# A masked softmax with lengths: masking 32 columns from the length on, with the tail filled by GpSimd

## The chip, the core and the metric

The kernel runs on one core of one Trainium2 chip. The metric is the device time of that core in microseconds (us): the median of several executions. The core has five engines that matter here: TensorE (PE), VectorE (DVE), ScalarE (ACT), GpSimd (POOL) and SyncE (SP), and 16 DMA engines that move data between the chip's main memory (HBM) and the on-chip memory (SBUF, 128 partitions). Engines run their own instruction streams and wait for one another through semaphores.

## What is computed

The input x is 16 x 8 x 256 x 256 in float32, with one length for each of the 16 batches. Each row of 256 columns gets a softmax over its first `length` columns; the columns behind are zero in the output.

```python
def reference(x, lengths):
    result = np.zeros_like(x)
    for b in range(batch):
        length = lengths[b]
        masked = x[b, :, :, :length].copy()
        masked = masked - np.max(masked, axis=-1, keepdims=True)
        exp_masked = np.exp(masked)
        result[b, :, :, :length] = exp_masked / np.sum(exp_masked, axis=-1, keepdims=True)
    return result
```

The lengths lie between 128 and 255. The draw that is timed has 188, 233, 229, 243, 195, 252, 165, 210, 222, 180, 209, 157, 159, 199, 214 and 248.

## The kernel before

A batch is 8 x 256 = 2048 rows, 16 on each of the 128 partitions: 16 x 256 float32, 16 KB on a partition and 2 MB in all. SBUF has `slots = 8` places for a batch (tile `xt`), and position b of the order uses slot b % 8. The order is batches 1, 2, 3, 15, then 4 to 14, and batch 0 last; `batch_of` maps positions to batches. `half`, `quarter` and `lump` are 8, 4 and 4 of a partition's 16 rows. Everything is written by hand with semaphores; no scheduler moves an instruction.

**Loads.** Position 0 is loaded by SP in two halves (L145). GpSimd loads positions 1 to 3 whole (L196), and then, in a loop over two parities, positions 4 to 15 (L205 to L211). For these it reads the length into a register (L210, by the helper at L135) and picks one of twelve loads by a tree of branches: `pick` has the widths 160, 168, ... 240 and 256, and its leaf loads only the first w columns of each row (L168). Before such a load GpSimd waits for the store that empties the slot (`s_st`, L209; the first four find it counted already by a seed) and for the landing of the load of the same parity before it (`s_sw`, L167). So two loads are under way at a time.

The columns w to 255 of the slot are not written by a narrow load. In slots 4 to 7 they are zeroed once at the start (L191, columns 160 to 255, four memsets); later they hold what the batch eight positions earlier left there, which are finite numbers.

**Mask.** For each position VectorE replaces t in columns 128 to 255 (`mid` to 255) by the smaller of t and `down + len_s` (L248, the function `clip`). `down` is -1e30 x (column + 0.5), `len_s` is 1e30 x length, so the sum is hugely negative from the column `length` on and hugely positive ahead of it. The function `mask` waits for the load and runs the clip over all 16 rows of a partition, 2048 elements (position 0 in two parts of 1024).

**Exponentials and sums.** ScalarE takes the exponential of the first 4 rows at once (L374), and of the other 12 one by one with their sums (L377). VectorE sums the first 4 rows (L269, `total`). No maximum is subtracted; at the end the sums are looked at, and if one lies outside a range (or a length is under 128) a slow path works all batches again. With this input it isn't taken.

**Division and stores.** VectorE multiplies each half of a batch by the reciprocal of its sums (L279 and L282, `divide`). Its order for position b is: divide the first half of b, mask b + 1, divide the second half of b, sum the lump of b + 1 (position 1 divides first what it can). SP stores the finished parts (L154): it waits for the part (`s_out`, L149) and, for positions 2 to 12, also for the complete store of position b - 2 (L153), so that two batches are in store at most; positions 13 to 15 wait for nothing else than their parts. At the end SP waits for all stores (L157 to L159, L407).

The helper `step` counts instructions of VectorE in the semaphore `s_v`; GpSimd waits for it at L188, ahead of its first memset of `xt` and of the loads of positions 1 to 3.

Of the kernel before, what the change touches and what calls it, by code (L numbers as in the profile page):

```python
# [9 lines left out]
F32 = mybir.dt.float32  # L10
BF16 = mybir.dt.bfloat16
I32 = mybir.dt.int32
ALU = mybir.AluOpType
AX = mybir.AxisListType.X
EXP = mybir.ActivationFunctionType.Exp
DVE = mybir.EngineType.DVE
# [5 lines left out]
def kernel(  # L22
# [6 lines left out]
    nc = tc.nc  # L29
    P = nc.NUM_PARTITIONS  # L30

    batch, heads, seq_q, seq_k = x.shape
    rows = heads * seq_q
    assert rows % P == 0
    nt = rows // P
# [10 lines left out]
    slots = 8  # L46
    ahead = 4
    assert ahead == 4 and slots == 8 and batch == 16

    def batch_of(pos):  # L50
        return pos + 1 if pos < ahead - 1 else {ahead - 1: 15, 15: 0}.get(pos, pos)
# [3 lines left out]
    low = widths[0]  # L55
    mid = seq_k // 2
    big = 1.0e30

    def parts(b):


        if b == 0:
            cuts = [0, 2, quarter, half, nt]
        elif b < 8:
            cuts = [0, half, half + quarter, nt]
        elif b < 13 or b == batch - 1:
            cuts = [0, half, nt]
        else:
            cuts = [0, nt]
        return [slice(i, j) for i, j in zip(cuts, cuts[1:])]  # L70

    pool = ctx.enter_context(tc.tile_pool(name="all", bufs=1))
    psum = ctx.enter_context(tc.tile_pool(name="psum", bufs=1, space=bass.MemoryType.PSUM))
    xt = pool.tile([P, slots, nt, seq_k], F32, name="xt")
    word64 = pool.tile([1, batch], mybir.dt.int64, name="word64")
    word = word64.bitcast(I32)
# [3 lines left out]
    len_s = pool.tile([P, batch], F32, name="len_s")  # L80
    iota_i = pool.tile([P, seq_k], I32, name="iota_i")
    down = pool.tile([P, seq_k], F32, name="down")
    row_sum = pool.tile([P, slots, nt], F32, name="row_sum")
    inv_sum = pool.tile([P, batch, nt], F32, name="inv_sum")
    warm = pool.tile([P, 1], F32, name="warm")
# [20 lines left out]
    with tc.tile_critical(no_gpsimd_drain=True):  # L106
# [9 lines left out]
        s_fill = sem("s_fill")  # L116
        s_v = sem("s_v")
        s_min = sem("s_min")
# [14 lines left out]
        def length(engine, at):  # L133

            return nc.values_load(  # L135
                at,
                engines=[engine],
                skip_runtime_bounds_check_because="compared with constants, never an address",
            )
# [3 lines left out]
        for h in range(2):  # L143
            s = slice(h * half, (h + 1) * half)
            nc.sync.dma_start(out=xt[:, 0, s], in_=x_f[batch_of(0), :, s]).then_inc(s_ld[h], 16)  # L145
        for b in range(batch):
            s_b = s_st[b % 2] if b < late else s_late if b < batch - 1 else s_last
            for s in parts(b):
# [3 lines left out]
                if 2 <= b < late and s.start == 0:  # L152
                    nc.sync.wait_ge(s_b, 64 * (b // 2 + 2))  # L153
                nc.sync.dma_start(  # L154
                    out=out_f[batch_of(b), :, s, :], in_=xt[:, b % slots, s, :]
# [7 lines left out]
        def pick(v, b, slot, par, ws, landed):  # L163

            if len(ws) == 1:
                w = ws[0]
                nc.gpsimd.wait_ge(s_sw[par], landed)  # L167
                nc.gpsimd.dma_start(  # L168
                    out=xt[:, slot, :, :w], in_=x_n[:, b, :, :w]
                ).then_inc(s_sw[par], 16)  # L170
                return
            m = (len(ws) - 1) // 2
            with nc.gpsimd.If(v <= ws[m]):
                pick(v, b, slot, par, ws[: m + 1], landed)
            with nc.gpsimd.Else():
                pick(v, b, slot, par, ws[m + 1 :], landed)
# [8 lines left out]
        nc.gpsimd.memset(ones_c, 1.0).then_inc(s_ones, 1)  # L185
        for par in range(2):
            nc.gpsimd.memset(seed[:, par : par + 1], 0.0).then_inc(s_st[par], 128)  # L187
        nc.gpsimd.wait_ge(s_v, 2)  # L188

        def fill(b):  # L190
            nc.gpsimd.memset(xt[:, b, :, low:], 0.0).then_inc(s_fill, 1)  # L191


        fill(ahead)
        for b in range(1, ahead):
            nc.gpsimd.dma_start(out=xt[:, b], in_=x_f[batch_of(b)]).then_inc(  # L196
                s_sw[b - 1] if b < 3 else s_ld[2], 16
            )
        nc.gpsimd.wait_ge(s_word, 16)
        for b in range(ahead + 1, slots):  # L200
            fill(b)
        nc.gpsimd.wait_ge(s_fill, slots - ahead)


        with nc.Fori(16, 16 * (batch // 2 - 1), 16, engines=[POOL]) as landed:  # L205
            for par in range(2):
                n = landed // 8 + (ahead - 2 + par)
                b = n % 15 if par == 1 else n
                nc.gpsimd.wait_ge(s_st[par], 4 * landed)  # L209
                v_len = length(POOL, word[0:1, bass.ds(2 * b, 1)])  # L210
                pick(v_len, bass.ds(b, 1), bass.ds(n % slots, 1), par, widths + [seq_k], landed)  # L211
# [11 lines left out]
        def step(ins):  # L223
            nonlocal v
            v += 1
            ins.then_inc(s_v, 1)
# [5 lines left out]
                out=down, in0=iota_i, scalar1=0.5, scalar2=-big, op0=ALU.add, op1=ALU.mult  # L232
            )
        )
        nc.vector.wait_ge(s_word, 16)
        nc.vector.tensor_copy(out=len_b, in_=word[:, ::2]).then_inc(s_lenb, 1)  # L236
        nc.vector.wait_ge(s_lenf, 1)
        step(
            nc.vector.tensor_scalar(  # L239
                out=len_s, in0=len_f, scalar1=big, scalar2=None, op0=ALU.mult  # L240
# [1 line left out]
        )  # L242
        nc.vector.wait_ge(s_v, v)

        def clip(b, s, lo, hi):

            t = xt[:, b % slots, s, lo:hi]
            return nc.vector.scalar_tensor_tensor(  # L248
                out=t,
                in0=down[:, None, lo:hi].to_broadcast([P, s.stop - s.start, hi - lo]),  # L250
                scalar=len_s[:, batch_of(b) : batch_of(b) + 1],
                in1=t,
                op0=ALU.add,
                op1=ALU.min,
            )

        def mask(b, s):
            if b == 0:
                nc.vector.wait_ge(s_ld[s.start // half], 16)
            elif b == ahead - 1:  # L260
                nc.vector.wait_ge(s_ld[2], 16)
            else:
                par = (b - 1 if b < ahead else b) % 2
                nc.vector.wait_ge(s_sw[par], 16 * max(b // 2, 1))
            clip(b, s, mid, seq_k).then_inc(s_min, 1)

        def total(b):
            nc.vector.wait_ge(s_lump, b + 1)
# [7 lines left out]
        def divide(b, h):  # L276
# [10 lines left out]
            ).then_inc(s_out, 1)  # L287

        mask(0, slice(0, half))
        mask(0, slice(half, nt))  # L290
        total(0)
        for b in range(batch):


            first = b != 1
            if first:
                divide(b, 0)
            if b + 1 < batch:
                mask(b + 1, slice(0, nt))
            if not first:  # L300
                divide(b, 0)
            divide(b, 1)
            if b + 1 < batch:
                total(b + 1)
# [14 lines left out]
        for k, (_, _, edge, op) in enumerate(checks):  # L319
            nc.vector.tensor_scalar(  # L320
                out=bad[:, k : k + 1],
                in0=ends[:, k : k + 1],
                scalar1=edge,
                scalar2=None,
                op0=op,
# [9 lines left out]
        with nc.vector.Else():  # L335
            with nc.Fori(0, batch, 1, engines=[DVE]) as i:
                nc.vector.wait_ge(g_ld, 16 * i + 16)
                nc.vector.scalar_tensor_tensor(
                    out=g_t,
                    in0=down[:, None, :].to_broadcast([P, nt, seq_k]),  # L340
                    scalar=len_s[:, bass.ds(i, 1)],
                    in1=g_t,
                    op0=ALU.add,
                    op1=ALU.min,
# [3 lines left out]
                    out=neg_max, in_=g_t, op=ALU.max, axis=AX, negate=True  # L348
# [5 lines left out]
                    out=g_t,  # L354
                    in0=g_t,
# [9 lines left out]
        with nc.Fori(0, batch // slots, 1, engines=[ACT]) as turn:  # L365
            for slot in range(slots):
                for h in range(2):
# [7 lines left out]
                    for j in range(h * half + lump * (1 - h), (h + 1) * half):  # L375
                        e = xt[:, slot, j, :]
                        ins = nc.scalar.activation(  # L377
                            out=e, in_=e, func=EXP, accum_out=row_sum[:, slot, j : j + 1]
# [5 lines left out]
        with nc.scalar.If(a_redo >= 1):  # L384
# [4 lines left out]
            with nc.Fori(0, batch, 1, engines=[ACT]) as i:  # L389
                nc.scalar.dma_start(out=g_t, in_=x_g[:, bass.ds(i, 1)]).then_inc(g_ld, 16)  # L390
                nc.scalar.wait_ge(g_v, 3 * i + 2)
                with nc.Fori(0, nt, 1, engines=[ACT]) as t:
                    e = g_t[:, bass.ds(t, 1), :]
                    nc.scalar.activation(
                        out=e,
                        in_=e,
# [41 lines left out]
```

## Time and profile before

| what | value |
|---|---|
| median of 3 runs | 154.53 us (154.44 to 154.55) |
| the profiled execution: from its first to its last instruction (span) | 152.8 us |
| between the span and the median of the runs | 1.7 us |
| VectorE busy | 134.6 us, 88% of the span |
| ScalarE busy | 95.1 us, 62% |
| GpSimd busy | 21.3 us, 14% |
| bytes moved by DMA | 61.57 MB, mean 403 GB/s |

The profiled execution is one run of its own and has no time beside its span; the time of the runs also has what lies ahead of the first and behind the last instruction. In rows of the profile, L282 is line 282 of the kernel; a row of instructions gives the line, the engine, the operation, output <- inputs with their shapes, then the busy time in us and the mean in ns of one, and the idle time before it with what ended it. "SPq" and "DVEq" are the sequencers of those engines, where waits, register instructions and DMA issues run, which are not counted as busy. A row of waits gives the waiter, what it waited for, us in total, times, and the longest. A row of stretches gives the window, its length, the busy time of PE, PEld, DVE, ACT and POOL with the number of instructions that began in it, the granted TensorE clock, the mean busy share of the 16 DMA engines (over 1 where packets overlap), and GB/s. q0 is the queue of GpSimd's loads, q1 that of SP's loads and stores.

### The profile page before, as it was taken

The numbers are of one execution on the slowest core, as the hardware profiler recorded it, in microseconds if no ns is written. First come the engines' busy times: TensorE is split into PE (matmuls) and PEld (weight loads), VectorE is DVE, ScalarE is ACT, GpSimd is POOL, SyncE is SP. The second block draws the span as 40 slices with busy tenths as digits, with TensorE's granted clock in tenths as the row PEclk, the third lists the DMA queues.
The fourth block names the chain that finished last, engine by engine and source line by source line (L and its number), as shares of the span: only waits on it lengthen the run. The fifth ranks groups of instructions, "written<-read, shape, count | busy, mean of one in ns | idle before, by whom it ended". The sixth has DMA issues, their size and how long they took to land.

```text
span 152.8 us, 818 instructions
## 1 busy us (share of the span) xinstructions
PE 0.3 (0%) x2; PEld 0.2 (0%) x2; DVE 134.6 (88%) x107; ACT 95.1 (62%) x402; POOL 21.3 (14%) x29
## 2 busy tenths in 40 slices
PE   0000000000000000000000000000000000000000
PEld 0000000000000000000000000000000000000000
DVE  1369999999999999999999999999999999999500
ACT  3096699339394967859393939577593939395000
POOL 4962110030303020030300220302000000000000
DMA  4999999999999999999999999999999999999994
GB/s 107 420 446 433 401 435 347 421 445 420 394 397 422 405 421 411 411 409 405 419 411 418 408 399 419 408 410 423 417 421 419 413 420 422 435 435 442 429 410 187
DMA packets 10646, 61.57 MB, mean 403 GB/s; under 512 B 898, under 2 KB 1010, under 8 KB 7058
## 3 DMA queue, kind: packets, MB, share of 16 engines
q1 hardware_dynamic: 5904, 35.65, 56.7%
q0 software_dynamic: 4736, 25.89, 41.9%
q14 instruction: 4, 0.03, 0.1%
q10 hardware_dynamic: 2, 0.00, 0.0%
HBM read 27.98 MB, written 33.55 MB: 403 GB/s over the span
## 4 chain that ended last, share of the span: by engine, by line
DVE 87%; DMA 5%; issue 1%; SPq 0%; PE 0%
DVE xt L282 48%; DVE xt L248 23%; DVE row_sum L269 12%; DMA xt<-in_x_dram 5%; DVE inv_sum L279 3%; DVE ends L317 0%; SPq L145 0%; DVE bad L320 0%; PE count L218 0%; DVE redo L328 0%; SPq L433 0%; SPq L106 0%
## 5 line engine op out<-in xcount | busy, mean ns | idle before, releaser
L377 ACT ACTIVATE xt<-xt 128x256 f32<-128x256 f32 x192 | 76.6, 400 | 0.2 <-DVE xt L248 0.2
L282 DVE TENSOR_TENSOR xt<-xt,inv_sum 128x2048 f32<-128x2048 f32 x32 | 73.3, 2292 | 1.1
L374 ACT ACTIVATE xt<-xt 128x1024 f32<-128x1024 f32 x16 | 16.9, 1056 | 42.8 <-DVE xt L248 42.8
L248 DVE SCALAR_TENSOR_TENSOR xt<-down,len_s,xt 128x2048 f32<-128x2048 f32 (+1 forms) x17 | 37.7, 2219 | 5.0 <-DMA xt<-in_x_dram 5.0
L377 ACT ACTIVATION_READ_ACCUMULATOR xt<-xt 128x1 f32 x192 | 35.9, 187 | 0.0
L168 POOL DMA_DIRECT2D xt<-in_x_dram x12 | 13.2, 1104 | 84.0 <-DMA xt<-in_x_dram 62.3
L269 DVE TENSOR_REDUCE row_sum<-xt 128x4 f32<-128x1024 f32 x16 | 19.4, 1210 | 0.0
L279 DVE RECIPROCAL inv_sum<-row_sum 128x8 f32<-128x8 f32 x32 | 6.3, 198 | 0.5
L191 POOL MEMSET xt<- 128x1536 f32 x4 | 5.4, 1398 | 1.1 <-DVE len_s L239 1.1
L361 ACT ACT_TABLE_LOAD x1 | 1.3, 1283 | 1.6 <-SPq L106 1.6
L196 POOL DMA_DIRECT2D xt<-in_x_dram x3 | 1.8, 590 | 0.0
L231 DVE TENSOR_SCALAR down<-iota_i 128x256 f32<-128x256 int32 x1 | 0.3, 300 | 1.6 <-POOL iota_i L181 1.6
L317 DVE TENSOR_REDUCE ends<-inv_sum 128x1 f32<-128x256 f32 x2 | 0.7, 408 | 0.0
L236 DVE CAST len_b<-word 1x16 bf16<-1x16 int32 x1 | 0.2, 164 | 0.4 <-DMA word<-in_lengths_dram 0.4
L239 DVE TENSOR_SCALAR len_s<-len_f 128x16 f32<-128x16 f32 x1 | 0.2, 176 | 0.3 <-PE len_f L216 0.3
L218 PE MATMUL count<-bad,ones_c 128*1 128x3 bf16 x1 | 0.2, 165 | 140.8 <-DVE bad L320 140.8
L181 POOL IOTA iota_i<- 128x256 int32 x1 | 0.3, 331 | 0.6 <-SPq L106 0.6
L328 DVE TENSOR_REDUCE redo<-count 1x1 f32<-1x3 f32 x1 | 0.1, 150 | 0.3 <-PE count L218 0.3
L320 DVE TENSOR_SCALAR bad<-ends 128x1 bf16<-128x1 f32 x3 | 0.3, 150 | 0.0
L187 POOL MEMSET seed<- 1x1 f32 x2 | 0.2, 225 | 0.0
L218 PEld LDWEIGHTS count<-bad,ones_c 128*1 128x1 bf16 x1 | 0.1, 79 | 140.8 <-DVE bad L320 140.8
L361 ACT ACTIVATE warm<-const-float32-0.0 128x1 f32<-128x1 f32 x1 | 0.2, 204 | 0.0
(10 smaller groups left out, 1.1 us busy)
## 6 DMA issues: line engine op xcount, KB each, us to landing
out_dram<-xt SPq DMA_DIRECT2D x20, 1024.0 KB
xt<-in_x_dram POOLq DMA_DIRECT2D x4, 2048.0 KB, 16.3
out_dram<-xt SPq DMA_DIRECT2D x15, 512.0 KB
xt<-in_x_dram POOLq DMA_DIRECT2D x3, 1728.0 KB, 16.7
out_dram<-xt SPq DMA_DIRECT2D x2, 2048.0 KB
xt<-in_x_dram POOLq DMA_DIRECT2D x2, 1600.0 KB, 16.0
xt<-in_x_dram POOLq DMA_DIRECT2D x2, 1280.0 KB, 14.7
xt<-in_x_dram SPq DMA_DIRECT2D x2, 1024.0 KB, 6.4
```

Of the source, the lines that this page charges most:

```text
L168: nc.gpsimd.dma_start(out=xt[:, slot, :, :w], in_=x_n[:, b, :, :w]).then_inc(s_sw[par], 16)
L191: nc.gpsimd.memset(xt[:, b, :, low:], 0.0).then_inc(s_fill, 1)
L196: nc.gpsimd.dma_start(out=xt[:, b], in_=x_f[batch_of(b)]).then_inc(s_sw[b - 1] if b < 3 else s_ld[2], 16)
L218: nc.tensor.matmul(count, lhsT=ones_c, rhs=bad, start=True, stop=True).then_inc(s_count, 1)
L248: return nc.vector.scalar_tensor_tensor(out=t, in0=down[:, None, lo:hi].to_broadcast([P, s.stop - s.start, hi - lo]), scalar=len_s[:, batc ...
L269: nc.vector.tensor_reduce(out=row_sum[:, b % slots, :lump], in_=xt[:, b % slots, :lump, :], op=ALU.add, axis=AX,).then_inc(s_exp[0], 1)
L279: step(nc.vector.reciprocal(out=inv_sum[:, b, s], in_=row_sum[:, b % slots, s]))
L282: nc.vector.tensor_tensor(out=t, in0=t, in1=inv_sum[:, b, s, None].to_broadcast([P, half, seq_k]), op=ALU.mult,).then_inc(s_out, 1)
L317: step(nc.vector.tensor_reduce(out=ends[:, k : k + 1], in_=values, op=op, axis=AX))
L361: nc.scalar.activation(out=warm, in_=nc.const_aps.tensor(0.0, (P, 1), F32), func=EXP)
L374: nc.scalar.activation(out=e, in_=e, func=EXP).then_inc(s_lump, 1)
L377: ins = nc.scalar.activation(out=e, in_=e, func=EXP, accum_out=row_sum[:, slot, j : j + 1])
```

## The change

- **Fill.** Behind each narrow load, `pick` has GpSimd copy -1e30 into the columns w to 255 of the slot, from a new tile `never` (128 x 96, set once at the start). For w = 256 it copies 16 elements into an unused tile instead, so that the semaphore `s_fill` counts each load. The memsets of slots 5 to 7 go; that of slot 4 stays, with -1e30 in place of 0.
- **Mask.** From position 4 on the mask covers 32 columns (`edge = low - mid`) from `min(length, 224)` on, in place of columns 128 to 255. The first column is computed for all batches at once by VectorE (`first_col`), read into a register of VectorE for each mask, and used as the offset into `xt` and `down`. Positions 0 to 3 keep the mask of columns 128 to 255.
- **Waits.** GpSimd's wait at the start asks for three counted instructions of VectorE, not two. The mask of position b from 4 on waits for the fill of its slot (`s_fill`) as well as for the load.

In the changed kernel's instruction stream each narrow mask is preceded on VectorE by one register load from SBUF and six register instructions. No DMA is added, removed or resized.

```diff
@@ -55,6 +55,7 @@
     low = widths[0]
     mid = seq_k // 2
     big = 1.0e30
+    edge = low - mid
 
     def parts(b):
 
@@ -80,6 +81,9 @@
     len_s = pool.tile([P, batch], F32, name="len_s")
     iota_i = pool.tile([P, seq_k], I32, name="iota_i")
     down = pool.tile([P, seq_k], F32, name="down")
+    never = pool.tile([P, seq_k - low], F32, name="never")
+    spent = pool.tile([P, nt], F32, name="spent")
+    first_col = pool.tile([1, batch], I32, name="first_col")
     row_sum = pool.tile([P, slots, nt], F32, name="row_sum")
     inv_sum = pool.tile([P, batch, nt], F32, name="inv_sum")
     warm = pool.tile([P, 1], F32, name="warm")
@@ -168,6 +172,11 @@
                 nc.gpsimd.dma_start(
                     out=xt[:, slot, :, :w], in_=x_n[:, b, :, :w]
                 ).then_inc(s_sw[par], 16)
+                m = max(seq_k - w, 1)
+                nc.gpsimd.tensor_copy(
+                    out=xt[:, slot, :, w:] if w < seq_k else spent[:, : nt, None],
+                    in_=never[:, None, :m].to_broadcast([P, nt, m]),
+                ).then_inc(s_fill, 1)
                 return
             m = (len(ws) - 1) // 2
             with nc.gpsimd.If(v <= ws[m]):
@@ -185,22 +194,16 @@
         nc.gpsimd.memset(ones_c, 1.0).then_inc(s_ones, 1)
         for par in range(2):
             nc.gpsimd.memset(seed[:, par : par + 1], 0.0).then_inc(s_st[par], 128)
-        nc.gpsimd.wait_ge(s_v, 2)
-
-        def fill(b):
-            nc.gpsimd.memset(xt[:, b, :, low:], 0.0).then_inc(s_fill, 1)
-
-
-        fill(ahead)
+        nc.gpsimd.wait_ge(s_v, 3)
+
+        nc.gpsimd.memset(xt[:, ahead, :, low:], -big).then_inc(s_fill, 1)
+        nc.gpsimd.memset(never, -big).then_inc(s_fill, 1)
         for b in range(1, ahead):
             nc.gpsimd.dma_start(out=xt[:, b], in_=x_f[batch_of(b)]).then_inc(
                 s_sw[b - 1] if b < 3 else s_ld[2], 16
             )
         nc.gpsimd.wait_ge(s_word, 16)
-        for b in range(ahead + 1, slots):
-            fill(b)
-        nc.gpsimd.wait_ge(s_fill, slots - ahead)
-
+        nc.gpsimd.wait_ge(s_fill, 2)
 
         with nc.Fori(16, 16 * (batch // 2 - 1), 16, engines=[POOL]) as landed:
             for par in range(2):
@@ -234,6 +237,16 @@
         )
         nc.vector.wait_ge(s_word, 16)
         nc.vector.tensor_copy(out=len_b, in_=word[:, ::2]).then_inc(s_lenb, 1)
+        step(
+            nc.vector.tensor_scalar(
+                out=first_col,
+                in0=word[:, ::2],
+                scalar1=seq_k - edge,
+                scalar2=0,
+                op0=ALU.min,
+                op1=ALU.max,
+            )
+        )
         nc.vector.wait_ge(s_lenf, 1)
         step(
             nc.vector.tensor_scalar(
@@ -242,12 +255,12 @@
         )
         nc.vector.wait_ge(s_v, v)
 
-        def clip(b, s, lo, hi):
-
-            t = xt[:, b % slots, s, lo:hi]
+        def clip(b, s, cols, n):
+
+            t = xt[:, b % slots, s, cols]
             return nc.vector.scalar_tensor_tensor(
                 out=t,
-                in0=down[:, None, lo:hi].to_broadcast([P, s.stop - s.start, hi - lo]),
+                in0=down[:, cols][:, None, :].to_broadcast([P, s.stop - s.start, n]),
                 scalar=len_s[:, batch_of(b) : batch_of(b) + 1],
                 in1=t,
                 op0=ALU.add,
@@ -255,6 +268,11 @@
             )
 
         def mask(b, s):
+            cols, n = slice(mid, seq_k), seq_k - mid
+            if b >= ahead:
+                k = batch_of(b)
+                cols, n = bass.ds(length(DVE, first_col[0:1, k : k + 1]), edge), edge
+                nc.vector.wait_ge(s_fill, b - ahead + 3)
             if b == 0:
                 nc.vector.wait_ge(s_ld[s.start // half], 16)
             elif b == ahead - 1:
@@ -262,7 +280,7 @@
             else:
                 par = (b - 1 if b < ahead else b) % 2
                 nc.vector.wait_ge(s_sw[par], 16 * max(b // 2, 1))
-            clip(b, s, mid, seq_k).then_inc(s_min, 1)
+            clip(b, s, cols, n).then_inc(s_min, 1)
 
         def total(b):
             nc.vector.wait_ge(s_lump, b + 1)
```

## The prediction

> **What bounds the kernel now.** I read the page first, its head, slices, queues and chain:
>
> ```profile
> span 152.8 us, 818 instructions
> ...
> PE 0.3 (0%) x2; PEld 0.2 (0%) x2; DVE 134.6 (88%) x107; ACT 95.1 (62%) x402; POOL 21.3 (14%) x29
> ...
> DMA  4999999999999999999999999999999999999994
> ...
> q1 hardware_dynamic: 5904, 35.65, 56.7%
> q0 software_dynamic: 4736, 25.89, 41.9%
> ...
> HBM read 27.98 MB, written 33.55 MB: 403 GB/s over the span
> ...
> DVE 87%; DMA 5%; issue 1%; SPq 0%; PE 0%
> ```
>
> Two resources look full. VectorE (DVE) is busy 88% of the span and owns 87% of the chain of waits. The 16 DMA engines are also busy, in 38 of 40 slices at 90% or more, and the two queues together took 56.7 + 41.9 = 98.6% of their span. The chain cannot tell which of the two sets the end, because its last instructions are VectorE's, and a store that is queued behind other stores does not show in it. So I ask the DMA side by stretches, with the columns DMA share and GB/s last:
>
> ```profile
> 0.00:2.00 2.00, 0.00 (x0) 0.00 (x0) 0.30 (x1) 0.35 (x1) 0.92 (x10) 1.00 0.00 0
> ...
> 5.00:10.00 5.00, 0.00 (x0) 0.00 (x0) 2.02 (x2) 2.22 (x8) 5.00 (x6) 1.00 1.04 441
> ...
> 35.00:127.00 92.00, 0.00 (x0) 0.00 (x0) 90.86 (x67) 63.98 (x275) 10.37 (x9) 1.00 1.02 413
> 127.00:149.00 22.00, 0.17 (x1) 0.08 (x1) 16.39 (x19) 10.21 (x47) 0.00 (x0) 1.00 1.01 429
> 149.00:153.00 4.00, 0.00 (x0) 0.00 (x0) 0.00 (x0) 0.00 (x0) 0.00 (x0) 1.00 0.42 178
> ```
>
> From 5 us to 149 us the DMA share is 1.01 or more: no engine of the 16 is without a packet. VectorE works 16.39 of the 22 us from 127 to 149 and is done; the DMA goes on past 149. What feeds the DMA, then? The waits of the queue that issues the stores (SP's), once from 34 to 128 us and once to the end:
>
> ```profile
> SPq L153 <- DMA out_dram<-xt: 86.6, 11, 9.9
> SPq L154 <- DVE xt L282: 1.1, 4, 0.5
> ...
> SPq L154 <- DVE xt L282: 13.1, 4, 7.6
> ```
>
> The first two rows are of 34 to 128 us. Eleven batches (2 to 12) wait 86.6 us for the store two batches earlier (L153), and only 1.1 us for VectorE's division (L154). Products lie ready, and the stores go out as fast as DMA drains them. The third row is of 127 to 153 us; there VectorE is waited for (batches 13 to 15), but with a backlog still in the queue. The loads:
>
> ```profile
> POOL xt L168 <- DMA xt<-in_x_dram: 62.3, 9, 12.9
> ...
> xt<-in_x_dram POOLq DMA_DIRECT2D x4, 2048.0 KB, 16.3
> ...
> xt<-in_x_dram POOLq DMA_DIRECT2D x3, 1728.0 KB, 16.7
> ...
> xt<-in_x_dram POOLq DMA_DIRECT2D x2, 1600.0 KB, 16.0
> xt<-in_x_dram POOLq DMA_DIRECT2D x2, 1280.0 KB, 14.7
> ...
> xt<-in_x_dram POOLq DMA_DIRECT2D x1, 1792.0 KB, 18.0
> xt<-in_x_dram POOLq DMA_DIRECT2D x1, 1536.0 KB, 21.0
> xt<-in_x_dram POOLq DMA_DIRECT2D x1, 1472.0 KB, 17.0
> xt<-in_x_dram POOLq DMA_DIRECT2D x1, 1344.0 KB, 13.4
> ...
> ...
> 106.21 1.15 POOL L168 DMA_DIRECT2D xt<-in_x_dram  x1 [6.97 <-issue]
> ```
>
> A load waits for the landing of the one two before it, and for the store of its slot; neither wait is for VectorE. The last load (batch 0; its length 188 makes 192 columns, the only load of 1536 KB) goes out at 106.2 and lands at 106.2 + 21.0 = 127.2 us. So **the DMA stream bounds the kernel**: from 35 us on its contents and order hang on its own completions, and VectorE runs beside it at nearly the same pace.
>
> **The change part by part.** Rows for the costs, the instructions by shape and then three sources:
>
> ```profile
> L248 DVE SCALAR_TENSOR_TENSOR xt<-down,len_s,xt 128x2048 f32<-128x2048 f32 x15 | 35.2, 2344 | 0.0
> L248 DVE SCALAR_TENSOR_TENSOR xt<-down,len_s,xt 128x1024 f32<-128x1024 f32 x2 | 2.6, 1284 | 5.0 <-DMA xt<-in_x_dram 5.0
> ...
> L135 DVEq TENSOR_LOAD <-redo x1: 842/842/842, 143.9 to 143.9; - x1
> ...
> L168 POOLq FUSED_REGOPS  x12: 102/107/116, 13.7 to 105.5; - x12
> ...
> L191 POOL MEMSET xt<- x4: 1387/1402/1403, 3.1 to 8.8; 128x1536 f32 x4
> ```
>
> *Mask.* Twelve of the 15 long masks (positions 4 to 15) shrink from 16x128 = 2048 elements to 16x32 = 512. Two lengths give the slope, (2344 - 1284) / 1024 = 1.035 ns an element, and a start of 224 ns; 512 elements are then 0.75 us, 1.59 us less. Each narrow mask also reads a register from SBUF (842 ns, VectorE's own row) and runs six register instructions (taken as the 107 ns of GpSimd's row: 0.64 us). Hidden beneath the multiplication before it, that costs nothing; fully exposed, it costs 1.48 us. So one mask saves between 1.59 and 0.11 us, twelve save 19.1 to 1.3 us of VectorE. I take no side, because the end does not depend on it: the division is not what the stores wait for before 128 us, and it may not start earlier than loads land. After that only batches 13 to 15 go out earlier, into a queue that is already full. **Gain: 0.**
>
> *Fill.* GpSimd writes seq_k - w columns after each load. The twelve loads of L168 (the rows above without three of the four of 2048 KB) move 19136 of 24576 KB, so the mean is 57 columns, 907 elements. The MEMSET row gives 1402 / 1536 = 0.91 ns an element: 0.8 us on the mean, 1.4 us at most. A copy also reads, which no row shows; between the memset's price and twice it lies 0.8 to 1.7 us on the mean, and 1.4 to 2.8 at most; I take the lower, nearest row. It begins after the load is issued and before GpSimd waits for the next. Cover:
>
> ```profile
> 14.52 1.17 POOL L168 DMA_DIRECT2D xt<-in_x_dram  x1 [4.36 <-DMA xt<-in_x_dram]
> 19.49 0.54 POOL L168 DMA_DIRECT2D xt<-in_x_dram  x1 [3.81 <-DMA xt<-in_x_dram]
> ...
> DMA to landing us min/median/max: 13.4/16.8/21.0
> ```
>
> The shortest idle before a load is 3.81 us, over the 2.8. The mask's new wait for the fill ends last only if the fill takes longer than the 13.4 us of the quickest landing. **Cost: 0.** Without that cover a load would be issued late by the excess, yet with another load and the stores in the queue no engine would run dry.
>
> *Start.* Three memsets (4.04 us, from 6.12) go; GpSimd waited 4.36 us behind them. The small first_col stands on VectorE's path to GpSimd's wait (2 becomes 3), and `never` (96 columns) stands ahead of the three full loads:
>
> ```profile
> 1.14 0.86 SPq L145 DMA_DIRECT2D xt<-in_x_dram  x2
> ...
> 2.82 0.18 DVE L239 TENSOR_SCALAR len_s<-len_f 128x16 f32<-128x16 f32 x1 [0.35 <-PE len_f L216]
> 3.05 1.39 POOL L191 MEMSET xt<- 128x1536 f32 x1 [1.11 <-DVE len_s L239]
> 4.37 1.76 POOL L196 DMA_DIRECT2D xt<-in_x_dram  x3
> ```
>
> first_col is of len_s's size, 0.18 us, and fits in the 0.35 us that VectorE idles for TensorE. `never` at 0.91 ns an element is 0.09 us, with a start as large as the mask's 0.3: 0.1 to 0.3 us. The loads of 4.37 leave that much later. Load 0 (2.10 MB, 4.8 us at 441 GB/s, nothing of it moved before 2.0 us) feeds the engines to 6.8 at least, so a gap opens only if the issue at 4.37 takes all of 2.4 us to its first packet. Cost 0, at most 0.3 us.
>
> *End.* What must not happen is that VectorE is later than the backlog. The last mask and the issue of the last half store:
>
> ```profile
> 131.53 2.34 DVE L248 SCALAR_TENSOR_TENSOR xt<-down,len_s,xt 128x2048 f32<-128x2048 f32 x1
> ...
> 142.46 0.36 SPq L154 DMA_DIRECT2D out_dram<-xt  x1
> ```
>
> The stream ends near 149 + 0.42 x 4 = 150.7 us. That half store (1.05 MB) takes 2.4 us at 429 GB/s, and some 1 us to start (load 0 was issued at 1.14 and moved nothing before 2.0): it could go out at 147.3, 4.8 us later, without a gap.
>
> *Sum.* 0 against the profiled span of 152.8 us; the median of the runs is 154.53, the 1.7 us between lying around the span. Forecast **154.5 us**, same.
>
> **The rivals.** (1) *Faster, VectorE is the bound after all.* The last mask could begin at 127.2, when its load lands, and not at 131.5 (it stands there in VectorE's order), and be 1.59 us shorter: 154.5 - 5.9 = 148.6 us. Against it: the DMA share of 1.02 from 35 to 127 us, and 1.1 us of waiting for VectorE. Chance 0.03.
>
> (2) *Faster, the packets speed up.* If 413 GB/s were low because of VectorE's traffic, the 92 us would shrink to 92 x 413 / 429 = 88.6 us: 151.1 us. For it: 429 GB/s where VectorE does less. Against: the narrow loads (5/8 to 7/8 of 2048 KB, so shorter rows) end at 127.2 too, and 441 GB/s stands in a stretch of whole rows. Chance 0.03. The Trainium skill, "DMA: Bandwidth & Descriptors", section "Where 436 GB/s comes from", puts the ceiling of the 16 ports at 435 GB/s; 61.57 MB at that rate would be an estimated 141.5 us. The trace's 441 over 5 us agrees that such a rate can be reached; no stretch of narrow loads shows it.
>
> (3) *Slower, the register path.* In VectorE's queue ahead of each narrow mask: a read of 842 ns, six register instructions, and perhaps a drain that no row shows. It decides once a mask takes 4.8 / 12 = 0.40 us more than its 2.34, so 2.74 us, against my 0.75 to 2.23. At 3.0 us the twelve add 7.9 us, of which 4.8 are covered: 157.6 us. Chance 0.05.
>
> (4) *Slower, fill and VectorE disturb each other.* If VectorE stands still for each fill and the register path is exposed as well, it loses 12 x (0.8 to 1.7) - 1.3 = 8 to 19 us, of which 4.8 are covered: 158 to 169 us. Against it: the four memsets took 1387 to 1403 ns alike, the first (3.05 us) with no mask beside it and later ones with the masks of load 0. Chance 0.03. The Trainium skill, "GPSIMD Engine Reference", section "Specifications", says that GpSimd shares its SBUF interfaces with VectorE, with contention where a VectorE instruction has two SBUF inputs, as mask and division have. The trace's memset shows none, but it reads nothing; a copy in SBUF is not shown here.
>
> (5) *Slower by little:* a start gap of 0.3 us plus packets that fills delay, 154.9 to 155.2. Against it: 441 GB/s from 5 to 10 us, with memsets all the while. Chance 0.04.
>
> **How the numbers follow.** Forecast 0.82, rivals 0.03, 0.03, 0.05, 0.03, 0.04. A measurement of this kernel can tell about 0.2%, 0.31 us, from no change. Faster 0.06, same 0.82, slower 0.12. The forecast's own range is 154.2 to 154.8; with the start gap and case (5) 154.2 to 155.0, which leaves out about 0.15.
>
> **What would show it.** In the changed kernel's profile the narrow mask reads 0.75 us, VectorE's busy time falls by some 19 us to about 115, and its share of the chain with it. VectorE gains idle time, waiting for loads, while the DMA share stays at 1.01 or more from 5 to 149 us with 413 GB/s from 35 to 127, the last load lands near 127, and the last division ends some us sooner without moving the end. I am wrong if the rate from 35 to 127 us changes, if a slice before 148 us falls under 9, or if the last half store is issued after 147 us.

## The result and the profile after

The changed kernel takes **155.36 us** (median of 9 runs, 155.23 to 156.45), the kernel before 154.53 us: a ratio of 1.0067, with a 95% interval of [1.0046, 1.0089]. It is slower by 0.8 us, and the forecast of 154.5 us (154.2 to 155.0) was wrong. The profiled execution's span is 153.5 us, against 152.8.

The page of the changed kernel: span, busy time, the slices of DMA, its queues with packets and MB, and the chain by engine.

```profile
span 153.5 us, 937 instructions
...
PE 0.3 (0%) x2; PEld 0.2 (0%) x2; DVE 126.0 (82%) x108; ACT 95.0 (62%) x402; POOL 38.3 (25%) x39
...
DMA  3999999999999999999999999999999999999992
...
q1 hardware_dynamic: 5904, 35.65, 56.4%
q0 software_dynamic: 4736, 25.89, 41.8%
q14 instruction: 6, 0.05, 0.1%
...
DMA 77%; DVE 7%; issue 3%; POOL 1%; POOLq 1%; DVEq 0%; PE 0%; ACTq 0%; SPq 0%
```

The chain has turned from VectorE to DMA, as it should where VectorE has slack. Loads and stores have the same packets and bytes as before. One row differs, the smallest of all: queue 14. On the page of the kernel before, it reads

```profile
q14 instruction: 4, 0.03, 0.1%
```

These are packets of 8 KB in which the engines' programs are fetched. Now the stretches that showed the bound, and SP's waits from 34 to 128 us (L157 and L158 are the old L153 and L154, L300 the division), both of the changed kernel:

```profile
35.00:127.00 92.00, 0.00 (x0) 0.00 (x0) 87.75 (x70) 68.38 (x297) 27.16 (x19) 1.00 1.02 412
127.00:149.00 22.00, 0.17 (x1) 0.08 (x1) 10.34 (x15) 5.85 (x25) 0.00 (x0) 1.00 1.01 428
149.00:153.00 4.00, 0.00 (x0) 0.00 (x0) 0.00 (x0) 0.00 (x0) 0.00 (x0) 1.00 0.45 188
```

```profile
SPq L157 <- DMA out_dram<-xt: 84.5, 11, 8.8
SPq L158 <- DVE xt L300: 2.5, 2, 2.1
```

412 GB/s against 413, and 428 against 429: the stream is the same, and VectorE is still not what the stores wait for. Its last division ends at 137.8 us in place of 142.4. So the 0.7 us of the span must lie at the very end. Two half-microseconds there, first of the kernel before, then of the changed one (DMA share and GB/s last):

```profile
151.00:151.50 0.50, 0.00 (x0) 0.00 (x0) 0.00 (x0) 0.00 (x0) 0.00 (x0) 1.00 0.01 0
151.50:152.00 0.50, 0.00 (x0) 0.00 (x0) 0.00 (x0) 0.00 (x0) 0.00 (x0) 1.00 0.00 0
```

```profile
151.00:151.50 0.50, 0.00 (x0) 0.00 (x0) 0.00 (x0) 0.00 (x0) 0.00 (x0) 1.00 0.08 33
151.50:152.00 0.50, 0.00 (x0) 0.00 (x0) 0.00 (x0) 0.00 (x0) 0.00 (x0) 1.00 0.04 16
```

16 GB/s for 0.5 us are 8 KB, one packet: after 151.5 us **one single DMA engine of the 16 is still at work**. In the records of single packets, the last data packet ends at 151.27 us before and at 151.97 after, which is the 0.7 us.

When did that engine fall behind? Each store ends with one completion mark from each of the 16 engines. In the kernel before, the last mark of a store lies 0.04 us behind the one before it, for all stores that end from 129 us on. In the changed kernel it is 0.04 us for the store that ends at 129 us, 0.27 at 132 us, 0.69 at 135 us, and 0.69 for every store from there to the end. The queues of the changed kernel from 131 to 133 us:

```profile
q1 hardware_dynamic: 117, 0.85, 102.2%
q14 instruction: 1, 0.01, 1.0%
```

A packet of the program is fetched there (at 131.70 us, for 0.31 us); the kernel before has none in these two us. The records of packets do not name their engine, so the tie is by time: the packet ends at 132.01 us, and at 132.01 us stands the first mark that is late. **Theory A**: the change makes VectorE's program longer (from 135 to 232 instructions, the slow path included: twelve times one register load, six register instructions and one wait, and first_col), so more of it is fetched while the kernel runs, and a fetch sets one of 16 full DMA engines back, for which the last store waits. **Rival B** (theory B in the expectations): the cause is on GpSimd's side, its longer program (from 140 to 185) or the writes of its fills. **Rival C**: the full loads, issued 0.15 us later at the start (4.52 against 4.37 us), leave a gap that is never made good.

### The profile page after: what moved, and what is told of

It is laid out like the page before. It is cut to its first block, busy times and chain, and to the rows that moved or that the text cites. A ratio compares the mean times of both kernels' runs of the same rounds, so it can differ in the third digit from the quotient of the medians.

```text
span 153.5 us, 937 instructions
## 1 busy us (share of the span) xinstructions
PE 0.3 (0%) x2; PEld 0.2 (0%) x2; DVE 126.0 (82%) x108; ACT 95.0 (62%) x402; POOL 38.3 (25%) x39
## 4 chain that ended last, share of the span: by engine, by line
DMA 77%; DVE 7%; issue 3%; POOL 1%; POOLq 1%; DVEq 0%; PE 0%; ACTq 0%; SPq 0%
DMA xt<-in_x_dram 77%; DVE xt L300 4%; POOL xt L199 1%; DMA word<-in_lengths_dram 1%; DVE row_sum L287 1%; POOLq L172 1%; DVE xt L261 0%; DVE ends L335 0%; DVE inv_sum L297 0%; DVEq L261 0%; POOLq L139 0%; DVE bad L338 0%; DVE len_s L252 0%; PE len_f L219 0%; PE count L221 0%
## 5 line engine op out<-in xcount | busy, mean ns | idle before, releaser
L300 DVE TENSOR_TENSOR xt<-xt,inv_sum 128x2048 f32<-128x2048 f32 x32 | 79.4, 2482 | 1.1
L261 DVE SCALAR_TENSOR_TENSOR xt<-down,len_s,xt (+2 forms) x17 | 22.7, 1336 | 9.1 <-DMA xt<-in_x_dram 5.4
L176 POOL COPY xt<-never 128x640 f32 (+6 forms) x11 | 18.7, 1699 | 0.0
L176 POOL COPY spent<-never 128x16 f32<-128x16 f32 x1 | 2.3, 2302 | 0.0
L199 POOL MEMSET xt<- 128x1536 f32 x1 | 1.4, 1388 | 1.1 <-DVE len_s L252 1.1
```

Source lines behind the costliest of these rows:

```text
L176: nc.gpsimd.tensor_copy(out=xt[:, slot, :, w:] if w < seq_k else spent[:, : nt, None], in_=never[:, None, :m].to_broadcast([P, nt, m]),).t ...
L199: nc.gpsimd.memset(xt[:, ahead, :, low:], -big).then_inc(s_fill, 1)
L261: return nc.vector.scalar_tensor_tensor(out=t, in0=down[:, cols][:, None, :].to_broadcast([P, s.stop - s.start, n]), scalar=len_s[:, batch ...
L300: nc.vector.tensor_tensor(out=t, in0=t, in1=inv_sum[:, b, s, None].to_broadcast([P, half, seq_k]), op=ALU.mult,).then_inc(s_out, 1)
```

## The experiments

All ratios are to the kernel before, with a 95% interval. Runs 1 and 2 leave out a part of the masking, as their expectations say; all other kernels compute what the reference does.

**1. Fixed columns, no registers.**

```diff
-                cols, n = bass.ds(length(DVE, first_col[0:1, k : k + 1]), edge), edge
+                cols, n = slice(seq_k - edge, seq_k), edge
```

> The changed kernel, but the narrow masks of positions 4 to 15 cover the fixed columns 224 to 255, so VectorE reads no register and runs no register instruction for them (its program has 148 instructions, against 232 of the changed kernel and 135 of the one before). The fills and GpSimd's longer program stay. Left out: the masking of the columns from the length on that lie ahead of 224 and ahead of the fill. Theory A (VectorE's longer program needs another instruction fetch, whose packets delay one of the full DMA engines): 2 fetch packets fewer on queue 14 than the changed kernel's 6, no lone DMA engine behind the others at the end, 154.5 us (154.3 to 154.8). Theory B (GpSimd's longer program does it, or its fills disturb the stream): 155.2 to 155.5.

Measured: 155.01 us, 1.0033 [1.0020, 1.0046], 5 packets on queue 14. Between the two. The step at 132 us is gone (the last mark is 0.03 to 0.17 us behind from 131 us to the end), so VectorE's program explains that step; some 0.5 us remain. For them stand B's two parts (GpSimd's longer program, which would be theory A for a second engine, or its fills) and C's late start, which this kernel keeps (full loads at 4.50 us).

**2. No fills.**

```diff
-                nc.gpsimd.tensor_copy(
-                    out=xt[:, slot, :, w:] if w < seq_k else spent[:, : nt, None],
-                    in_=never[:, None, :m].to_broadcast([P, nt, m]),
-                ).then_inc(s_fill, 1)
...
-                nc.vector.wait_ge(s_fill, b - ahead + 3)
```

> The changed kernel without the twelve copies of GpSimd behind the loads; the slots are set to -1e30 once, as the kernel before set them to zero. The narrow masks with their register reads stay (220 instructions of VectorE, 141 of GpSimd). Left out: the clearing of columns that a narrow load does not write. Theory A (VectorE's program): still 6 packets on queue 14 or so, a lone DMA engine late, 155.2 to 155.5 us. Theory B (GpSimd's program or its fills): 154.5 us.

Measured: 155.56 us, 1.0063 [1.0043, 1.0083]. Without a single fill the whole loss is there. Queue 14 has 5 packets, not 6; one goes at 132.8 us, and the last mark steps from 0.02 us behind (132 us) to 0.76 (135 us). The late start is kept here too (full loads at 4.49 us), so C is not excluded by this run.

**3. The kernel before with 96 idle instructions on VectorE.**

```diff
+            if b >= ahead:
+                for _ in range(16):
+                    nc.vector.wait_ge(s_ld[0], 16)
             clip(b, s, mid, seq_k).then_inc(s_min, 1)
```

> The kernel before, with 96 more instructions on VectorE: ahead of each mask from position 4 on, 8 instructions that wait for semaphores which are long past (231 instructions in VectorE's program). No fill, no register, no narrow mask. Theory A (length of VectorE's program): 6 packets on queue 14, a fetch in the last third, 155.1 to 155.5 us, although VectorE has only some us more to do. Theory B: 154.5 us. Should the waits themselves cost VectorE 0.05 us each, its last division ends 5 us later, near 147, which is about where the end would begin to move.

Measured: 155.21 us, 1.0043 [1.0030, 1.0056]. This kernel has nothing of the change but the length of VectorE's program, and it loses 0.7 us. Its page and its end:

```profile
q14 instruction: 5, 0.04, 0.1%
```

```profile
151.50:152.00 0.50, 0.00 (x0) 0.00 (x0) 0.00 (x0) 0.00 (x0) 0.00 (x0) 1.00 0.04 16
```

Again one packet more (at 133.9 us; I had expected two more), and again one engine alone after 151.5 us. The last mark steps from 0.06 to 0.78 us behind with the packet. (Two waits of the loop make one instruction; the trace has 96 of them, 50 ns each on VectorE's sequencer.) The 96 waits themselves hardly cost VectorE anything: it is busy for 134.6 us, as before, and its last half store begins 0.2 us later.

**4. The same with 48.** The loop of the edit above runs 8 times, not 16.

> As the run with 96 more instructions, with 48 (183 instructions in VectorE's program). Theory A with a fetch by blocks: VectorE does not reach the next block, 4 packets on queue 14, 154.5 us. If the cost grew with each instruction in place of by blocks: half of that of 96 more, 154.8 to 155.0. Theory B: 154.5 us.

Measured: 154.60 us, 1.0003 [0.9995, 1.0012]. Its page:

```profile
q14 instruction: 4, 0.03, 0.1%
```

Half of the instructions cost not half of the time but none. So the cost comes **by blocks**: with 183 instructions no further fetch, with 231 one (and with 220, in run 2, one). The Trainium skill, "Runtime: NRT & Kernel Launch", section "Instruction fetch mechanics", says that each engine's instruction memory is refilled in blocks (16 KiB, 256 instructions), by DMA while the current block runs, and that crossing a block costs little and is mostly hidden. The trace agrees on blocks and on DMA, but not on the size: the further fetch is one packet of 8 KB. The 0.7 us of run 3 speak against "mostly hidden" where the DMA engines are the bound.

**5. The kernel before with a longer GpSimd program.** In each leaf of the tree, behind the load:

```diff
+                for _ in range(4):
+                    nc.gpsimd.wait_ge(s_word, 16)
                 return
```

> The kernel before, with two more instructions in each of the 24 leaves of GpSimd's tree (waits that are long past): 188 instructions in GpSimd's program, against 140 before and 185 in the changed kernel; VectorE's program is that of before (135). No fill, no narrow mask. Theory A as it stands now (each program that grows past a block has one more fetch, and the fetch delays the DMA engine that carries it): a fifth packet on queue 14, near 151 us as in the run with fixed columns, and 154.8 to 155.1 us. Rival (the 0.3% of the run with fixed columns came from the fills' writes, not from GpSimd's program): 154.5 us.

Measured: 154.91 us, 1.0019 [1.0010, 1.0028], 5 packets on queue 14. A longer program of GpSimd costs time by itself. It can be the missing part of run 1: the intervals, 0.10 to 0.28% here and 0.20 to 0.46% there, overlap, and run 1 has its late start besides. The packet came at 23.7 us, not near 151 as expected. From the next store on one engine is late: by 1.15 us at 25 us (0.35 before), up to 1.6 around 50 us, 0.6 at 127, and 0.5 at the end. That it is the engine of the packet is likely by the time, not on record.

**6. A shorter mask.** Fixed comparison columns, and declared bounds for the register:

```diff
-                in0=down[:, cols][:, None, :].to_broadcast([P, s.stop - s.start, n]),
-                scalar=len_s[:, batch_of(b) : batch_of(b) + 1],
+                in0=down[:, None, base].to_broadcast([P, s.stop - s.start, n]),
+                scalar=lens[:, batch_of(b) : batch_of(b) + 1],
...
+                    min_val=0,
+                    max_val=seq_k - edge,
```

Here `base` is columns 0 to 31 for positions 4 to 15, and `lens` then holds 1e30 x max(length - 224, 0). VectorE computes it ahead of len_s, on which GpSimd waits at the start.

> The changed kernel, computing the same, with fewer instructions on VectorE: the narrow mask takes its comparison columns from fixed ones and a shifted length for each batch, and the register is loaded with declared bounds, which leaves one register instruction for each mask in place of six (174 instructions in VectorE's program). GpSimd as in the changed kernel (185, with fills). Theory A: VectorE's late fetch is gone, GpSimd's stays: 154.9 to 155.1 us, as with fixed columns. If register reads by VectorE cost by themselves: 155.3.

Measured: 155.63 us, 1.0066 [1.0054, 1.0079]. Neither forecast. The fetch at 132 us is gone (5 packets; the fifth at 151.7 us), but the two further instructions of VectorE at the start delay the full loads to 4.79 us, and less is moved behind them. The stretch from 7 to 9 us, first of the kernel before, then of this one (GB/s last):

```profile
7.00:9.00 2.00, 0.00 (x0) 0.00 (x0) 0.75 (x1) 1.22 (x2) 2.00 (x3) 1.00 1.07 455
```

```profile
7.00:9.00 2.00, 0.00 (x0) 0.00 (x0) 0.90 (x2) 1.08 (x2) 0.00 (x0) 1.00 1.10 401
```

54 GB/s less for 2 us are 0.11 MB, and it goes on: over the first 12 us the mean is 303 GB/s against 330, 0.32 MB less, 0.76 us at 429 GB/s. (The changed kernel has 328, 0.02 MB less.) That is rival C's mechanism, at 0.4 us of delay; runs 9 to 11 are about it. The profiled execution of this run, the slowest of its six, also ends with a lone engine, 0.64 us behind from 130 us on, and it was behind by 0.9 us at 25 us already, with no further fetch before 151.7 us. So a lone late engine at the end does not prove a fetch; the step at the time of a packet, as in the changed kernel and in runs 2 and 3, points to one.

**7. One fill ahead of each load.** With the shorter mask of run 6, in GpSimd's loop, the copies in the leaves and the memset of slot 4 removed. GpSimd waits for the fill ahead of the load, and so the mask no longer waits for it:

```diff
+                nc.gpsimd.tensor_copy(
+                    out=xt[:, bass.ds(n % slots, 1), :, low:],
+                    in_=never[:, None, None, :].to_broadcast([P, 1, nt, seq_k - low]),
+                ).then_inc(s_fill, 8)
+                nc.gpsimd.wait_ge(s_fill, landed + 8 * par)
```

> As the short version, and the fill is a single copy of columns 160 to 255 for each loaded batch ahead of its load, in place of one in each leaf behind it (GpSimd's program 145 instructions, VectorE's 162). It fills more: 1536 elements each time, while GpSimd waits for a landing anyway. It computes the same. Theory A (programs): 4 packets on queue 14, 154.5 us. Rival (the fills' writes into SBUF disturb the DMA stream or VectorE's end): 154.9 us or more, since more is filled than in the changed kernel.

Measured: 154.54 us, 1.0000 [0.9991, 1.0009]. It fills 1536 elements for each of the twelve loads, where the changed kernel copies 908 on the mean, and has the narrow masks and their register reads; nothing is lost. VectorE's divisions are held up by the copies as in the changed kernel (78.2 us against 73.3 before). Its page and its end:

```profile
q14 instruction: 4, 0.03, 0.1%
```

```profile
151.50:152.00 0.50, 0.00 (x0) 0.00 (x0) 0.00 (x0) 0.00 (x0) 0.00 (x0) 1.00 0.00 0
```

What was left of rival B, the fills, falls: they cost nothing where the programs are short. (Its full loads leave at 4.0 us, so there is no start gap either: 330 GB/s over the first 12 us, as before.)

**8. Larger stores, on the kernel before.**

```diff
-        elif b < 8:
-            cuts = [0, half, half + quarter, nt]
         elif b < 13 or b == batch - 1:
```

> The kernel before, but positions 1 to 7 store their second half in one piece in place of two quarters, so 8 KB lie together on a partition and not 4 KB. It asks whether the DMA stream really sets the end, and what its packets cost: 1920 packets of 4 KB at 163 ns become 960 of 8 KB at 315 ns, 11 us of packet time, 0.7 us for each of 16 DMA engines. If the DMA stream is the bound: 153.8 us (153.6 to 154.1), unless the loads, which take turns with the stores, land so much later that VectorE's end passes 147 us; then 154.5 or more. If VectorE were the bound: 154.5 us.

Measured: 158.28 us, 1.0254 [1.0232, 1.0277]. The warning in the expectation was the outcome, and worse than its "154.5 or more". The stretches of this kernel, and what its masks waited for:

```profile
35.00:127.00 92.00, 0.00 (x0) 0.00 (x0) 84.40 (x62) 59.54 (x257) 10.36 (x9) 1.00 1.01 415
127.00:150.00 23.00, 0.00 (x0) 0.00 (x0) 22.33 (x17) 14.91 (x67) 0.00 (x0) 1.00 0.86 347
```

```profile
DVE xt L246 <- DMA xt<-in_x_dram: 12.1, 8, 3.5
```

The counts of packets say that loads and stores take turns packet by packet: from 35 to 127 us the kernel before moves 3859 of loads and 3925 of stores, this one 3311 and 3251. With packets of 8 KB against the loads' 4.3 to 4.8 KB the stores get more of each round, 23.7 MB in that time and not 21.3. The last load lands at 137.5 us and not at 127.2, VectorE waits for loads, and from 127 us the DMA share falls to 0.86: engines run dry. The DMA bound holds only while the loads stay ahead. (1792 packets of 4 KB became 896, not 1920 becoming 960: those of position 0 stay.)

**9. The changed kernel with its early start.** The memset of `never` moves behind the three full loads.

> The changed kernel, but the tile of -1e30 is set behind the three full loads of the start, not ahead of them, so that they are issued near 4.4 us as in the kernel before and not at 4.5. The result is the same. Theory A (the two longer programs are the cost): 155.1 to 155.4 us, a lone DMA engine late from about 132 us. Rival C (loads 0.15 us later at the start leave engines idle between 7 and 9 us, and that is the cost): 154.5 to 154.8 us.

Measured: 155.19 us, 1.0048 [1.0035, 1.0061]; issue at 4.38 us, packets on queue 14 at 131.6 and 151.2 us, the last mark steps from 0.08 us behind (129 us) to 0.58 (135 us), and is 0.35 behind at the end. So most of the loss is not the start's. The 0.17 us less than the changed kernel could be the start's (434 GB/s from 7 to 9 us there, 455 before: 0.04 MB, 0.1 us), but the two intervals overlap.

**10. The shorter mask with the early start.** As run 6, but the shifted lengths are computed behind len_s, and `never` is set behind the full loads.

> The short version (narrow mask with one register instruction, 174 instructions of VectorE), with the three full loads issued near 4.4 us; in the short version they left at 4.8, and DMA engines stood idle for 1.9 engine-us between 7 and 9 us. It computes the same. If that start gap was why the short version took 155.63 and not 155.0: 154.9 to 155.1 us here, what GpSimd's longer program costs. If register reads by VectorE cost the time: 155.5 or more.

Measured: 155.02 us, 1.0043 [1.0027, 1.0058]; issue at 4.37 us. The start gap of run 6 was worth 0.6 us. What is left equals run 1, and GpSimd's longer program fits: the last mark is 0.01 us behind up to the store that ends at 149 us and 0.28 at the last one, with a packet of queue 14 at 150.8 us. The profiled execution is the fastest of the six (154.78 us) and shows no more than this.

**11. The start gap alone.** Run 7 with the memset of slot 4 ahead of the full loads:

```diff
+        nc.gpsimd.memset(xt[:, ahead, :, low:], -big).then_inc(s_fill, 8)
```

> The version with one fill ahead of each load (154.54 us, full loads issued at 4.0 us), with the memset of slot 4 put back ahead of the three full loads, so that they leave near 4.9 us. It measures the start gap by itself: programs are short (147 and 162 instructions). If a late issue leaves DMA engines idle at 7 to 9 us and the end follows: 155.0 to 155.6 us. If not: 154.5 us.

Measured: 155.25 us, 1.0045 [1.0032, 1.0058], with 4 packets on queue 14 and issue at 4.85 us. From 7 to 9 us, first of run 7, then of this kernel:

```profile
7.00:9.00 2.00, 0.00 (x0) 0.00 (x0) 1.33 (x1) 0.64 (x1) 0.24 (x1) 1.00 1.14 483
```

```profile
7.00:9.00 2.00, 0.00 (x0) 0.00 (x0) 2.00 (x1) 0.00 (x0) 1.07 (x1) 1.00 0.90 332
```

Here the share falls under 1: 0.85 us later than run 7 costs 0.7 us, and 332 against 483 GB/s for 2 us, 0.30 MB, are 0.70 us at 429 GB/s. The late start leaves the engines unequal too: with no further fetch the last mark is 0.30 us behind from 130 us to the end. The point from which a delay costs clearly lies between 4.4 and 4.8 us.

**12. Run 7 with whole stores at the end.** Positions 12 and 15 are stored in one piece.

```diff
-        elif b < 13 or b == batch - 1:
+        elif b < 12:
```

> The version with one fill ahead of each load, and positions 12 and 15 are stored whole like 13 and 14 (16 KB on a partition together, 611 ns for 16 KB and not 2 x 309 to 315). From 127 us no load takes turns with the stores, and with the narrow masks VectorE is done near 138 us, so that nothing waits for a half. 512 packets fewer save 16 to 30 ns each pair, 0.3 us for each engine: 154.2 us (154.1 to 154.4) if the DMA stream is the bound; 154.5 if something else is.

Measured: 154.65 us, 1.0009 [0.9994, 1.0023]; no gain. The saving was sized with the packets of the mixed stretch. Where only stores run, 8 KB take 309 ns, half of the 611 of 16 KB but for 3.5 ns: 256 pairs at 7 ns are 0.1 us an engine, too little to be seen here. No version here beats the kernel before; run 7 equals it.

## Why the prediction was wrong

- **What bounds the kernel** was right, and it is why a change of VectorE's work gained nothing: 412 GB/s against 413, the last load at 127.4 us against 127.2, the last division 4.6 us sooner, the end not sooner. (One reading was too wide: from 20 to 30 us the DMA share was 0.99, at 391 GB/s, not 1.01.) None of my three signs of being wrong came: the rate held, no slice but the first and the last is under 9, and the last half store went out at 137.9 us. They watched the whole stream, while the loss sat on one engine.
- **The mask.** Where no copy runs beside it the narrow mask takes 0.74 to 0.75 us (estimate 0.75), and the register path is hidden. In the changed kernel, two masks in order of time, and the register reads of VectorE (ns least, median, most):

```profile
56.12 0.74 DVE L261 SCALAR_TENSOR_TENSOR xt<-down,len_s,xt  x1
...
85.89 1.95 DVE L261 SCALAR_TENSOR_TENSOR xt<-down,len_s,xt  x1
```

```profile
L139 DVEq TENSOR_LOAD <-first_col x12: 311/444/971, 39.3 to 122.6; - x12
```

  The multiplication ahead of the first begins at 53.91 and takes 2.29 us; the mask follows at 56.12 without a gap. The second ran beside a copy.
- **The fill** was cheaper in the sum than it was: 1.70 us a copy on the mean, at the upper end of my 0.8 to 1.7 and not at the lower that I took, and 3.05 us at most, over my 2.8. It stayed covered (least idle before a load 2.75 us).
- **Rival 4's mechanism is real, its price was covered.** Copies of GpSimd and instructions of VectorE with two inputs hold each other up. Groups of the changed kernel, and one pair in order of time (the two rows of each engine are of its own timeline):

```profile
L300 DVE TENSOR_TENSOR xt<-xt,inv_sum 128x2048 f32<-128x2048 f32 x32 | 79.4, 2482 | 1.1
...
L261 DVE SCALAR_TENSOR_TENSOR xt<-down,len_s,xt x12 | 13.1, 1093 | 4.5 <-issue 3.7 <-DMA xt<-in_x_dram 0.9
```

```profile
33.36 4.50 DVE L300 TENSOR_TENSOR xt<-xt,inv_sum 128x2048 f32<-128x2048 f32 x1
```

```profile
34.33 1.37 POOL L176 COPY xt<-never 128x1408 f32 x1
...
107.35 3.05 POOL L176 COPY xt<-never 128x1024 f32 x1
```

  A division of 2.29 us takes 4.50 beside a copy; the 32 divisions take 79.4 us, not 73.3, and the masks 13.1 us, not 12 x 0.75 = 9.0. So VectorE got 8.6 us lighter and not 19. The Trainium skill's rule that I cited from the "GPSIMD Engine Reference", section "Specifications", is shown here: a copy contends where the memset had not. It moved no end: run 7 has it too and loses nothing.
- **The start** was put at 0, at most 0.3 us, for loads 0.1 to 0.3 us later. They were 0.15 us later, and run 9 leaves about 0.2 us for it, not clear of noise. That it stayed small was partly luck. I had tied a gap to 2.4 us from issue to first packet; in the kernel before it took 3.3 us (4.37 to 7.67) and no gap showed, because load 0 ran slower than my 441 GB/s and fed the engines to 8.4 us, not 6.8. Beyond the slack the price is higher than I had bounded it: issued 0.42 us later, run 6 took 0.61 us longer than run 10.
- **The step that failed** is the sum itself, "0 against the profiled span": it holds no term for fetching longer programs, some 0.7 us. I counted time of the added instructions on their engines, found it covered, and forgot that instructions are also bytes which the full DMA engines must fetch. "No DMA is added" was true of the kernel's text alone; the queue's row, q14, stood on the page and I did not read it. By itself VectorE's longer program costs 0.43% (run 3), GpSimd's 0.19% (run 5), and both together, as in run 9, 0.48% [0.35, 0.61]. That the two do not simply add up would fit an end that follows the latest engine and not the sum, but the sum, 0.62%, lies at the edge of the interval, so it is not shown. With both programs short nothing is lost (run 7).
- **The chances.** "Slower" had 0.12, its parts with other mechanisms than the one that decided; the range ended at 155.0, and even the case "slower by little", at 155.2.

Left open: two of the nine runs of the changed kernel took 156.45 us, and one of the eight of run 2, which has the same late start, but none of the five of run 9; a start gap in those runs would fit, but no profile of them exists. Why one fetch costs more than another, and more than its packet's own time, is seen, not explained (below).

## What to carry to other kernels

When all DMA engines are full to the end, count what an edit adds in program length, not only in engine time: find the row of the instruction queue, and see whether the last store waits for one engine alone. Unrolled code with six register instructions for each mask, and one copy in each leaf of a tree, were the dear forms here; one register instruction for each mask and one fill in the loop (run 7) were free. And a chain of waits that names one engine at 87% is no proof of a bound, if a queue beside it never runs empty.

## What the runs showed of the hardware that I had not expected

- One fetch packet of 8 KB takes 0.31 us by its record, but with it an engine falls back by some 0.7 us (0.04 to 0.69 us behind in the changed kernel, 0.06 to 0.78 in run 3, 0.02 to 0.76 in run 2) or 0.5 (run 9). With the one near 151 us in run 10 it was 0.27 only, near the packet's own length.
- While loads and stores are mixed, a lone engine's delay can shrink: in the kernel before from 0.33 us at 65 us to 0.02 at 103, in run 5 from 1.6 to 0.6. It need not: in run 6 it was 1.00 us at 66 us and 1.18 at 124. In the stretch of stores alone, from 127 us, it stays at 0.69 in the changed kernel, and goes from 0.78 to 0.67 in run 3 and from 0.58 to 0.35 in run 9.
- The full loads of the start need 3 us and more from issue to first packet, and an issue ahead of 4.5 us brought no earlier packet: issued at 4.01 us (run 7), 4.37 (before) and 4.52 (changed), the first packets came at 7.68, 7.67 and 7.60 us; issued at 4.79 (run 6) and 4.85 (run 11), at 7.86 and 7.83.
